# First four row tiles of x in four pieces of the contraction, w1 ahead of w2, three w sums on GpSimd

## The chip, the cores and the metric

The kernel runs on one core of a Trainium2 chip. The metric is the device time of one execution in microseconds (us). Before the change three runs took 298.63, 298.87 and 299.97 us; the median, 298.87 us, is the number to be forecast for the changed kernel.

## The reference

```python
def setup_inputs():
    batch, m, k, n = 16, 512, 1024, 768
    return {
        "x": np.random.randn(batch, m, k).astype(np.float32),
        "w1": np.random.randn(k, n).astype(np.float32),
        "w2": np.random.randn(k, n).astype(np.float32),
    }

def reference(x, w1, w2):
    y1 = np.matmul(x, w1)
    y2 = np.matmul(x, w2)
    return (np.tanh(y1) * y2).astype(np.float32)
```

Seen as one matrix, x has 8192 rows, that is 64 row tiles of 128 rows, with a contraction of 1024, that is 8 pieces (k = 0 to 7) of 128. Both w1 and w2 have 768 columns. Everything is multiplied in 16-bit floats and summed in 32-bit floats.

## The kernel before

**Blocks.** In the code `u` is w1 and `v` is w2; `u3` is the 128 contraction rows k = 3 of w1, 128 partitions by 768 columns, 384 KB. The columns of the result are cut into three blocks of 512: `a` is columns 0 to 511 of x·w1, `b` is columns 0 to 511 of x·w2, and `G` holds the last 256 columns of both, side by side. One matmul instruction multiplies a 128x128 piece of transposed x with 128x512 of w and adds into one of the eight banks of PSUM; four of them (half of the contraction) are a slot.

**The head.** The first four row tiles (`HEAD = 4`) are computed plainly: for each tile eight matmuls for `a`, eight for `b`, eight for `G`, 88 in all, because the `b` block of tile 3 is kept back and done as the last thing of the kernel. The head exists to give TensorE work while w1 and w2 are still arriving. Its row tiles come by four loads of 512 KB in 32-bit floats (`y0` to `y3`, lines 411 to 415), are cast to 16 bits (line 417), transposed by TensorE, eight 128x128 transposes for a tile (line 460), and copied out of PSUM into tiles `xT` in two halves of 512 columns (line 465).

**The rest.** The other 60 row tiles are done as 20 triples. In a triple the three tiles' two contraction halves are six x blocks, named by bits: 1 and 2 are the halves of the first tile, 4 and 8 of the second, 16 and 32 of the third. The six w blocks are named the same way: 1, 2, 4 are `a`, `b`, `G` of contraction half 0 (k = 0 to 3), and 8, 16, 32 are `a`, `b`, `G` of half 1 (k = 4 to 7). A table of sums and differences lets 15 products do the work of 18. `A_SUMS` are sums of x blocks, one VectorE instruction on 128x512 16-bit values each (line 507), made anew for each triple. `B_SUMS` are eleven sums of w blocks, one VectorE instruction on 128x2048 16-bit values each (line 497), made once and kept. `C_OPS` is the list of products (`p0` to `p14`, four matmuls each, line 550), of copies and additions between PSUM banks and SBUF, and of the tanh and multiply at the end. The first triple needs the w sums first.

**The planner.** `Planner` lays out all operations by a list schedule: each has a duration for each engine that may do it, a due time, and what it needs. The matmuls of the head may be put in any order that fits; the products run in the fixed order `plan.strict`. The first triple's products of this order are, before the change, p7 p1 p6 p10 p9 p12 p8 p11 p14, then p7 of the second triple, then p0 and p13 of the first. The order that the planner finds is pinned: each engine's instructions run in it, and each queue issues its loads in it.

**Loads.** `SP_LOADS` and `ACT_LOADS` are the orders in which SyncE and ScalarE issue the loads of the four row tiles and of the sixteen pieces of w. Row tiles 4, 5 and 6, and after them all others, are loaded by GpSimd's queue with a cast on the way (line 471). The first of these is held back by a `gate`, a one-element GpSimd copy that reads a freshly landed w piece (`POOL_LOADS = "5.0:v5 ..."` waits for v5); later ones are paced by `gate_x`, a one-element GpSimd copy of transposed x (line 586). Tiles 4, 5 and 6 are transposed by TensorE, those from 7 on by a DMA transpose on SyncE's queue (line 474). Every piece of w is cast to 16 bits by ScalarE or VectorE (lines 427 and 429).

**Warm-up.** Before the first load lands, TensorE multiplies constants (`WARM`), and at four places that are named by hand (`FILLERS`) it does so again in a wait of the head.

Of the kernel before, what the change touches and what calls it, by code (L numbers as in the profile page):

```python
# [85 lines left out]
MUL_DUE = 0.022  # L86
MARGIN = {"S": 0.407, "B": 0.262, "T": 5.87, "L": 9.71, "early": 0.060}
# [3 lines left out]
FILLERS = {"PT1.0": (512,), "m1b2": (192,), "m1b7": (256,), "PT2.1": (448,)}  # L91
# [5 lines left out]
SP_LOADS = ("y0 y1 v7 u3 y2 u1 v4 u0 v0 "  # L97
            "v1 v3 u2 u4 v5 v6 u6 u5 u7")
ACT_LOADS = "y3 v2"
POOL_LOADS = "5.0:v5 4.0 4.1 5.1 6"  # L100


class Planner:
# [221 lines left out]
    def spare(self, n):  # L325

        t = self.start_of[n]
        return [b for b in range(len(self.held)) if all(t <= a or z <= t - 1.0 for a, z in self.held[b])][0]
# [3 lines left out]
def kernel(  # L332
# [7 lines left out]
    nc = tc.nc  # L340
# [19 lines left out]
    XF_BUFS, XG_BUFS = 3, max((SP_LOADS + ACT_LOADS).count("y"), 1)  # L360
# [13 lines left out]
    xtpool = pool("xt", XT_BUFS)  # L374
# [15 lines left out]
    xt_last = once.tile([P, KO, P], f16, name="xT_last")  # L390
# [7 lines left out]
    xgpool = head_stack.enter_context(tc.tile_pool(name="xg", bufs=XG_BUFS))  # L398
# [12 lines left out]
    def load_x32(e, mt, halves):  # L411
        if mt not in x32:
            x32[mt] = xfpool.tile([P, K], f32, tag="xf", name="x_f")
        at = slice(halves[0] * F, (halves[-1] + 1) * F)
        pin(engine[e].dma_start(x32[mt][:, at], xf[mt][:, at]))  # L415

    def cast_y(e, mt):
        xhs[mt] = xgpool.tile([P, K], f16, tag="xh", name="xh")
        copy(e, xhs[mt], x32[mt])
# [27 lines left out]

    def xt_tile(mt):
        if mt not in xts:
            xts[mt] = xt_last if mt == HEAD - 1 else xtpool.tile([P, KO, P], f16, tag=f"xT{mt % 3}", name="xT")  # L450
        return xts[mt]

    def transpose_32(e, mt, h, chain):
        for k in range(KH):
            pin(nc.tensor.transpose(bank(chain)[:, k * P:(k + 1) * P], x32[mt][:, (h * KH + k) * P:(h * KH + k + 1) * P], ident))

    def evacuate_32(e, mt, h, chain):
        copy(e, xt_tile(mt)[:, h * KH:(h + 1) * KH, :].rearrange("p k m -> p (k m)"), bank(chain))
# [9 lines left out]
    def load_x(e, mt, lo, n):  # L468
        if mt not in xhs:
            xhs[mt] = (xgpool if mt < HEAD else xhpool).tile([P, K], f16, tag="xh", name="xh")  # L470
        pin(nc.gpsimd.dma_start(xhs[mt][:, lo * P:(lo + n) * P], xf[mt][:, lo * P:(lo + n) * P]))  # L471
# [7 lines left out]
    def abs_x(e, mt):  # L479
        abs_sum(e, xhs[mt] if mt in xhs else x32[mt], mt)  # L480
# [18 lines left out]
    def x_operand(i, v):  # L499
        if v & (v - 1):  # L500
            return ss[i, v]
        bit = v.bit_length() - 1
        return xts[HEAD + 3 * i + bit // 2][:, bit % 2 * KH:(bit % 2 + 1) * KH, :]
# [15 lines left out]
    def mm(e, chain, mt, k, c, lo, n):  # L519
        begun[chain] = begun.get(chain, 0) + 1  # L520
        w = w_columns(k, c, lo, n)
        pin(nc.tensor.matmul(shaped(bank(chain)[:, lo:lo + n], w), xts[mt][:, k, :], w, start=begun[chain] == 1, stop=begun[chain] == KO, skip_group_check=True))  # L522

    def plain_tanh(e, mt, lo, n, chain):
        pin(nc.scalar.activation(out_tile(mt)[:, lo:lo + n], bank(chain)[:, :n], ACT.Tanh))
# [59 lines left out]
    def gate_x(e, mt):  # L585
        pin(nc.gpsimd.tensor_copy(held_x, xts[mt][:, 0, :1]))  # L586

    def gate(e, c, k):
        pin(nc.gpsimd.tensor_copy(held, (x32[k] if c == "y" else wfs[c, k])[:, :1]))
# [7 lines left out]
    K_ORDER = [4, 5, 6, 7, 0, 1, 2, 3]  # L597

    head = PE_HEAD.split()
    head_at = {entry: HEAD_START + n * SLOT for n, entry in enumerate(head)}  # L600
    ORIGIN = HEAD_START + (len(head) - 15) * SLOT
# [25 lines left out]
    parts, early, last, back = {}, set(), "", []  # L627
    both = sorted([(ISSUE_ACT * z, "act", z, n) for z, n in enumerate(act_loads)] + [(ISSUE_SP * z, "sp", z, n) for z, n in enumerate(sp_loads)])
    issuer, last_on = {}, {"act": "", "sp": ""}
    for _, e, z, n in both:  # L630
# [3 lines left out]
        if n[1] == "y":  # L634
            mt = int(n[2])
            op(n, {e: (0.49, 0.49) if e == "sp" else (ISSUE_ACT, 0.5) if n != act_loads[-1] else (ISSUE_ACT + TABLE, 0.5)}, -100, [], load_x32, mt, (0, 1), issued=[last], behind=back[-WF_BUFS:][:1] if len(back) >= WF_BUFS else [],
               dma=(e, 1.295 + more, 1.15, 0.75, 0.159))
            op(f"cy{mt}", {"dve": (0.6, 0.69), "act": (0.92, 1.02)}, None, [n], cast_y, mt)
            back.append(f"cy{mt}")
            for h in range(2):  # L640
                parts.setdefault(mt, []).append((h * KH, KH))
                op(f"PT{mt}.{h}", {"pe": (0.25, 0.25)}, None, [f"cy{mt}"], transpose_16, mt, h * KH, KH, ("T", mt, h), chains=[("T", mt, h)])
                op(f"T{mt}.{h}", {"dve": (0.36, 0.45), "act": (0.51, 0.6)}, None, [f"PT{mt}.{h}"], evacuate_16, mt, h * KH, KH, ("T", mt, h), chains=[("T", mt, h)])
                early.add(f"T{mt}.{h}")
        elif n[1] == "x":
# [334 lines left out]
```

## Time and profile before

| what | value |
|---|---|
| runs (us) | 298.63, 298.87, 299.97; median 298.87 |
| span of the profiled execution, first to last instruction | 297.3 us |
| median less that span | 1.6 us |
| TensorE busy | 290.9 us, 98% of the span |
| VectorE busy | 255.5 us, 86% |
| ScalarE busy | 227.6 us, 77% |
| GpSimd busy | 46.7 us, 16% |

The profiled execution has no time of its own in the list of runs; its span stands beside the median, and the 1.6 us between them lie ahead of the first and behind the last instruction, as far as the two executions are alike. The span counts from its first instruction, and all places in the trace are given in us from there. PE is TensorE, PEld its loads of the stationary operand, DVE VectorE, ACT ScalarE, POOL GpSimd, SP SyncE. A row of the timeline has its start, its length, the engine, the line, the operation with output and input, and how many instructions it merges; in brackets stands how long the engine had been idle before it and what ended that. Matmuls are pipelined, so the length of one is longer than the distance to the next.

### The profile page before, as it was taken

What the parts mean: (1) busy time and instruction counts of PE and PEld (TensorE: products, weight loads), DVE (VectorE), ACT (ScalarE), POOL (GpSimd) and SP (SyncE); (2) the same over time, 40 slices, a digit from 0 to 9 for tenths busy, and PEclk for the clock granted to TensorE, in tenths of its full rate; (3) what the DMA queues carried; (4) which work ended last, traced back from release to release, by engine and by line L of the source; (5) the groups of instructions that cost most, each with busy time, mean ns of one, the idle gap of its engine ahead of it and who ended that gap; (6) DMA issues with size and microseconds to landing.
All of it is one profiled execution on the core that took longest, in us unless ns stands there. A gap on an engine that the chain in (4) does not pass through costs nothing.

```text
span 297.3 us, 4698 instructions
## 1 busy us (share of the span) xinstructions
PE 290.9 (98%) x1419; PEld 137.7 (46%) x1419; DVE 255.5 (86%) x517; ACT 227.6 (77%) x450; POOL 46.7 (16%) x122
## 2 busy tenths in 40 slices
PE   6999999999999999999999999999999999999995
PEld 3545444444444675444444444444444444444443
DVE  1458999999988999898899988989899898999685
ACT  3798988996969769697876979788696866867561
POOL 1024040211030111113121010212101030000000
PEclk9999999999999999999999999999999999999999
DMA  7999999999999999999999999999989899681316
GB/s 263 406 403 230 162 169 222 242 251 258 110 317 212 221 255 244 221 215 259 161 227 217 172 223 199 246 224 215 226 169 245 164 279 244 144 240 47 119 55 215
DMA packets 82827, 64.55 MB, mean 217 GB/s; under 512 B 62704, under 2 KB 64752, under 8 KB 82800
## 3 DMA queue, kind: packets, MB, share of 16 engines
q1 hardware_dynamic: 73584, 47.59, 62.6%
q0 software_dynamic: 8928, 15.73, 34.3%
q10 hardware_dynamic: 288, 0.92, 0.8%
q8 instruction: 11, 0.18, 0.3%
q14 instruction: 16, 0.13, 0.1%
HBM read 39.85 MB, written 25.17 MB: 219 GB/s over the span
## 4 chain that ended last, share of the span: by engine, by line
PE 91%; DMA 6%; ACT 1%; SPq 0%; DVE 0%; issue 0%
PE bank L550 87%; DMA w_f<-in_w_dram 4%; PE bank L522 3%; DMA x_f<-in_x_dram 2%; ACT wh L427 1%; PE bank L463 1%; SPq L423 0%; DVE o_last L529 0%; SPq L415 0%; PE bank L580 0%
## 5 line engine op out<-in xcount | busy, mean ns | idle before, releaser
L550 PE MATMUL bank<-b,s 128*128 128x512 f16 (+1 forms) x664 | 148.1, 371 | 0.0
L550 PEld LDWEIGHTS <-s 128*128 128x128 f16 x832 | 81.2, 98 | 91.4 <-DVE s L507 0.6
L553 ACT ACTIVATE s<-bank 128x512 f32<-128x512 f32 x100 | 58.6, 595 | 41.0 <-PE bank L550 40.5
L560 DVE TENSOR_TENSOR bank<-bank,s 128x512 f32<-128x512 f32 x100 | 69.5, 697 | 18.1 <-PE bank L550 7.8
L477 ACT ACTIVATE junk<-xh 128x1024 f16<-128x1024 f16 x64 | 67.3, 1051 | 0.2
L567 DVE TENSOR_TENSOR o<-o,bank 128x512 f32<-128x512 f32 (+1 forms) x120 | 63.1, 548 | 2.5 <-ACT o L563 1.7
L550 PEld LDWEIGHTS <-xT 128*128 128x128 f16 x412 | 40.3, 98 | 46.1 <-ACT xT L427 0.2
L550 PE MATMUL bank<-b,xT 128*128 128x512 f16 (+1 forms) x252 | 58.5, 369 | 0.0
L563 ACT ACTIVATE o<-bank 128x256 f32<-128x256 f32 (+1 forms) x80 | 33.0, 432 | 12.4 <-PE bank L550 6.1
L550 PE MATMUL bank<-wh,s 128*128 128x512 f16 (+1 forms) x168 | 41.1, 369 | 0.0
L550 PE MATMUL bank<-wh,xT 128*128 128x512 f16 x160 | 40.9, 379 | 0.0
L586 POOL COPY held_x<-xT 128x1 f16<-128x1 f16 x52 | 12.2, 235 | 165.1 <-DMA xT<-xh 165.0
L471 POOL DMA_DIRECT2D xh<-in_x_dram x62 | 33.3, 540 | 20.3 <-issue 6.6
L507 DVE TENSOR_TENSOR s<-s,xT 128x512 f16<-128x512 f16 x80 | 32.3, 421 | 1.2
L563 ACT ACTIVATE o<-s 128x512 f32<-128x512 f32 x40 | 24.9, 623 | 1.2 <-DVE s L560 1.2
L507 DVE TENSOR_TENSOR s<-xT 128x512 f16<-128x512 f16 x60 | 25.0, 418 | 0.0
L553 ACT ACTIVATE bank<-bank 128x512 f32<-128x512 f32 x40 | 21.7, 573 | 1.6 <-DVE bank L560 0.9
L522 PE MATMUL bank<-wh,xT 128*128 128x512 f16 x72 | 18.8, 378 | 0.3
L507 DVE TENSOR_TENSOR s<-xT,s 128x512 f16<-128x512 f16 x40 | 16.7, 417 | 0.0
L560 DVE TENSOR_TENSOR bank<-s,bank 128x512 f32<-128x512 f32 x20 | 13.9, 694 | 1.6
L560 DVE TENSOR_TENSOR s<-s,bank 128x512 f32<-128x512 f32 x20 | 13.6, 681 | 0.3 <-ACT s L553 0.3
L477 ACT ACTIVATE junk<-wh 128x768 f16<-128x768 f16 x16 | 13.5, 842 | 0.2
(42 smaller groups left out, 120.6 us busy)
## 6 DMA issues: line engine op xcount, KB each, us to landing
out_dram<-o SPq DMA_DIRECT2D x54, 384.0 KB, 4.7
xh<-in_x_dram POOLq DMA_DIRECT2D x58, 256.0 KB, 5.7
w_f<-in_w_dram SPq DMA_DIRECT2D x15, 384.0 KB, 6.3
out_dram<-o SPq DMA_DIRECT2D x9, 256.0 KB, 2.0
x_f<-in_x_dram SPq DMA_DIRECT2D x3, 512.0 KB, 4.7
out_dram<-o SPq DMA_DIRECT2D x9, 128.0 KB, 1.7
xT<-xh SPq DMA_TRANSPOSE x57, 5.3
x_f<-in_x_dram ACTq DMA_DIRECT2D x1, 512.0 KB, 4.9
```

Of the source, the lines that this page charges most:

```text
L427: pin(nc.scalar.copy(dst, src))
L463: pin(nc.tensor.transpose(b[:, (k - lo) * P:(k - lo + 1) * P], xhs[mt][:, k * P:(k + 1) * P], ident_h))
L471: pin(nc.gpsimd.dma_start(xhs[mt][:, lo * P:(lo + n) * P], xf[mt][:, lo * P:(lo + n) * P]))
L477: pin(nc.scalar.activation(junk[:, :src.shape[-1]], src, ACT.Abs, scale=scale, accum_out=sums[:, column:column + 1]))
L507: pin(engine[e].tensor_tensor(ss[i, v], x_operand(i, a), x_operand(i, b), OP[how]))
L522: pin(nc.tensor.matmul(shaped(bank(chain)[:, lo:lo + n], w), xts[mt][:, k, :], w, start=begun[chain] == 1, stop=begun[chain] == KO, skip_g ...
L550: pin(nc.tensor.matmul(to, x_operand(i, a)[:, k, :], w, start=begins and k == 0, stop=k == KH - 1, skip_group_check=True))
L553: pin(nc.scalar.activation(place(i, dst, True), place(i, src), ACT.Copy, scale=float(sign)))
L560: pin(nc.vector.tensor_tensor(d, a, b, ALU.add if signs == (1, 1) else ALU.subtract))
L563: pin(nc.scalar.activation(out_tile(HEAD + 3 * i + r)[:, lo:lo + n], place(i, src)[:, :n], ACT.Tanh, scale=float(sign)))
L567: pin(nc.vector.tensor_tensor(o, o, place(i, src)[:, at:at + n], ALU.mult))
L586: pin(nc.gpsimd.tensor_copy(held_x, xts[mt][:, 0, :1]))
```

## The change

The four row tiles of the head are no longer loaded tile by tile. A load `q0` to `q3` now brings two of the eight contraction pieces (256 columns, 1 KB of each row) of all four tiles together, 512 KB as before; one cast makes 16 bits of it, eight transposes turn it, and one copy of 1024 columns brings it out of PSUM for all four tiles. So the head can use a piece of w for all four tiles as soon as the matching `q` is there. The loads come in a new order: q0 and q2 early, q1 and q3 behind the first six pieces of w1, and all of w1 but u6 and u1 ahead of w2; v7 and v6 are last. The gate of the row tiles from 4 on waits for v3. The head's `G` is split in `U` (w1's last 256 columns) and `V` (w2's), 256 columns each, two row tiles to a bank. Three of the eleven w sums, 26 = 2 − 24, 37 = 1 − 36 and 27 = 29 − 6, go from VectorE to GpSimd. The products of the first triple begin with p1 and p6 in place of p7. All transposed x lies in one tile with the same number of places as before. The planner's margins are new, and the filling multiplications are put by rule wherever the plan has a wait.

```diff
-PE_HEAD = ("1a0 0a1 1b1 0b1 1G1 p7 p1 0a0 3a0 2b1 p6 0G0 2a1 1b0 1G0 3a1 "
-           "p10 3G1 0b0 p9 p12 2G1 p8 1a1 p11 p14 2b0 0G1 3G0 2G0 2a0")
-HEAD_START = 2.5
+PE_HEAD = ("1a1 p1 p6 0U1 0a1 2a0 3V0 1U0 1V0 3a0 3U1 1a0 2U1 0U0 3V1 p7 p10 2V1 2V0 p9 0V0 0a0 1b0 "
+           "2U0 1U1 0b0 2a1 1b1 p12 p8 3U0 2b1 p11 3a1 2b0 0V1 p14 0b1 1V1")
+HEAD_START = 14.142
...
-MUL_DUE = 0.022
-MARGIN = {"S": 0.407, "B": 0.262, "T": 5.87, "L": 9.71, "early": 0.060}
+MUL_DUE = 2.735
+MARGIN = {"S": 1.925, "B": 0.146, "T": 14.795, "L": 4.568, "early": 0.268}
...
-FILLERS = {"PT1.0": (512,), "m1b2": (192,), "m1b7": (256,), "PT2.1": (448,)}
...
-SP_LOADS = ("y0 y1 v7 u3 y2 u1 v4 u0 v0 "
-            "v1 v3 u2 u4 v5 v6 u6 u5 u7")
-ACT_LOADS = "y3 v2"
-POOL_LOADS = "5.0:v5 4.0 4.1 5.1 6"
+SP_LOADS = "u5 q2 u4 u0 u7 u2 q1 q3 v2 u6 v0 u1 v1 v3 v4 v5 v7 v6"
+ACT_LOADS = "q0 u3"
+XQ, XQ32, XQ_GROUPS = (2, 2, 2, 2), (), 1
+POOL_B = (26, 37, 27)
+POOL_LOADS = "4.1:v3 6 5.1 5.0 4.0"
...
+    def fillers(self, until):
+        found, busy = {}, None
+        for n in sorted((n for n in self.ops if self.engine_of[n] == "pe"), key=lambda n: self.start_of[n]):
+            t = self.start_of[n]
...
+            if busy is not None and t - busy > 0.32 and self.spare(n):
+                found[n] = self.spare(n)[0], int((t - busy - 0.12) * 600) // 32 * 32
+            busy = t + self.ops[n]["engines"]["pe"][0]
+        return found
...
+    xt_all = once.tile([P, HEAD + 3 * (XT_BUFS - 1), KO, P], f16, name="xT")
...
+    def load_q(e, j):
+        k, w = xq_at[j]
+        x32[j] = xfpool.tile([P, HEAD, w * P], f32, tag="xf", name="x_f")
+        pin(engine[e].dma_start(x32[j], xf[:HEAD].rearrange("mt p k -> p mt k")[:, :, k * P:(k + w) * P]))
+
+    def cast_q(e, j):
+        k, w = xq_at[j]
+        copy(e, xh_head[:, :, k * P:(k + w) * P], x32[j])
...
+    def transpose_q(e, j, g, chain):
+        k, w = xq_at[j]
+        n = HEAD // XQ_GROUPS
+        b = bank(chain) if j in XQ32 else bank(chain).bitcast(f16)
+        for mt in range(n):
+            for z in range(w):
+                src = x32[j][:, g * n + mt, z * P:(z + 1) * P] if j in XQ32 else xh_head[:, g * n + mt, (k + z) * P:(k + z + 1) * P]
+                pin(nc.tensor.transpose(b[:, (mt * w + z) * P:(mt * w + z + 1) * P], src, ident if j in XQ32 else ident_h))
+
+    def evacuate_q(e, j, g, chain):
+        k, w = xq_at[j]
+        n = HEAD // XQ_GROUPS
+        b = bank(chain) if j in XQ32 else bank(chain).bitcast(f16)
+        copy(e, xt_all[:, g * n:(g + 1) * n, k:k + w, :], b[:, :n * w * P].rearrange("p (t k m) -> p t k m", t=n, k=w))
...
+    def mm(e, chain, mt, k, c, lo, n, at, count):
         begun[chain] = begun.get(chain, 0) + 1
+        col = N * (c in "bV") + F * (c in "UV") + lo
+        pin(nc.tensor.matmul(bank(chain)[:, at:at + n], xt_tile(mt)[:, k, :], wh[:, k, col:col + n], start=begun[chain] == 1, stop=begun[chain] == count, skip_group_check=True))
...
     for v, a, b, how in B_SUMS:
-        op(f"B{v}", {"dve": DVE_B}, None, w_needs(a) + w_needs(b), w_sum, v, a, b, how)
+        op(f"B{v}", {"pool": (4.6, 4.7)} if v in POOL_B else {"dve": DVE_B}, None, w_needs(a) + w_needs(b), w_sum, v, a, b, how)
...
+    fillers = plan.fillers(24.0)
```

More of the change, by code (lines that the diff above doesn't have):

```diff
@@ L711 @@
[L711 removed]
+                took = MM if n == F else MM / 2
+                op(name, {"pe": (took, took)}, head_at[f"{mt}{c}{k // KH}"] + z % KH * took, [f"c{'uv'[c in 'bV']}{k}", part(mt, k)],
+                   mm, chain, mt, k, c, 0, n, lo, KO if c in "ab" else 2 * KO, chains=[chain])
+                plain[c, mt].append(name)
+            xt_readers[mt] += plain[c, mt]
+    for c in "aUbV":
+        for mt in range(HEAD):
+            if (c, mt) not in plain:
+                continue
```

157 lines of the change are left out of this document (77 added, 80 removed).

## The prediction

> **What bounds the kernel now.** I read the page first, then the chain of waits, then the timeline of the first 45 us. The page's first and fourth parts say that TensorE is busy for 98% of the span and makes 91% of the chain that ended last. In the chain in order of time (start, length, what; the second fence) no other engine and no transfer releases TensorE after 22.98:
>
> ```profile
> span 297.3 us, 4698 instructions
> ...
> PE 290.9 (98%) x1419; PEld 137.7 (46%) x1419; DVE 255.5 (86%) x517; ACT 227.6 (77%) x450; POOL 46.7 (16%) x122
> ...
> PE 91%; DMA 6%; ACT 1%; SPq 0%; DVE 0%; issue 0%
> ```
>
> ```profile
> 22.98 3.40 PE bank L522 x15
> ...
> 36.63 242.78 PE bank L550 x1168
> 279.41 0.01 PE bank L580
> 279.42 12.97 PE bank L550 x60
> 292.38 1.76 PE bank L522 x16
> ```
>
> The 1168 products from 36.63 on include 44 extra ones (the sixth triple's eleven products that do not begin a bank are cut in halves), so they are 1124 matmuls of 512 columns: 0.216 us each. Nothing is left to win there. Only the head can move, and a delay in it goes to the end undiminished. The rows of the head:
>
> ```profile
> 9.16 0.38 PE L522 MATMUL bank<-wh,xT 128*128 128x512 f16 x1
> ...
> 12.45 0.62 PE L463 MATMUL bank<-ident_h,xh 128*128 128x128 f16 x8
> ...
> 24.12 0.56 DVE L429 CAST wh<-w_f 128x768 f16<-128x768 f32 x1 [0.90 <-DMA w_f<-in_w_dram]
> ...
> 26.38 0.40 PE L463 MATMUL bank<-ident_h,xh 128*128 128x128 f16 x4
> ...
> 40.66 1.55 PEld L550 LDWEIGHTS <-xT 128*128 128x128 f16 x8 [0.18 <-DMA xT<-xh]
> 40.82 1.03 PE L550 MATMUL bank<-wh,xT 128*128 128x512 f16 x4
> ...
> 41.68 1.03 PE L550 MATMUL bank<-b,xT 128*128 128x512 f16 x4
> ```
>
> The first matmul on data starts at 9.16. By 36.47 TensorE has done the 88 plain matmuls and four products, 104 matmuls, or 22.5 us, and 32 transposes of 0.056 us (0.45 us of spacing for eight), 1.8 us. The stretch is 27.3 us, so TensorE waited 3.0 us in it, filling partly with constants. The product at 41.68 is p0 of the first triple, the one with a single x block against a w sum (27); the one before it, at 40.82, is p7 of the second triple, which just found its transposed x tile. I use 41.68 as the anchor: p0 needs sum 27, and the order of products is fixed, so what p0 loses the kernel loses.
>
> **The head's gain.** Transfers go at one rate whatever the order:
>
> ```profile
> 4.00:6.00 2.00, 1.21 (x4) 0.53 (x2) 0.10 (x1) 0.30 (x1) 0.00 (x0) 1.00 1.02 416
> ...
> 18.00:20.00 2.00, 2.00 (x10) 0.88 (x9) 1.70 (x2) 1.97 (x6) 0.00 (x0) 1.00 1.03 399
> ```
>
> ```profile
> out_dram<-o SPq DMA_DIRECT2D x9, 256.0 KB, 2.0
> out_dram<-o SPq DMA_DIRECT2D x9, 128.0 KB, 1.7
> ```
>
> ```profile
> 7.95 0.69 DVE L429 CAST xh<-x_f 128x1024 f16<-128x1024 f32 x1
> ```
>
> (First two stretches of 2 us, whose last number is GB/s; then two stores with their us from issue to landing; then a cast of a row tile.) Before, y0, y3, y1 and v2 (1.97 MB) lay ahead of the cast at 7.95 or beside it. After, q0, u5, q2 and u3 (1.84 MB) come first, so q2 with u5 is there at about 7.8. Then follow the cast 0.69, eight transposes 0.62, and one copy of 1024 columns, about 0.8 on VectorE: the first matmul at 9.9, that is **+0.75**. From there each piece of w1 gives 4 x 1.5 matmuls, 1.3 us, while 384 KB at 400 GB/s take 0.98 us. u5, u4 and u0 keep TensorE busy for 3.9 us, to 13.8. The next piece needs q1, the seventh load on SyncE's queue. By bytes it lands at about 13.1, and with its cast, transposes and copy it is usable at 15.3: of these 1.5 us the transposes take 0.45, and 1.0 is waiting. q3 follows inside the work of u3 and u2. Waiting falls from 3.0 to 1.0, **-2.0**. Eight more transposes fall behind the first matmul, **+0.45**, and 64 matmuls of 256 columns at 0.110 (1.76 for 16) in place of 32 at 0.216 cost **+0.1**. Together -0.7: without anything else p0 comes at 41.0. Bounds: all waiting gone and the start kept, -2.5; the start late by another 1 us and the waiting kept, +2.
>
> The four q loads have rows of 1 KB in place of 4 KB. No load of before has such rows; the stores above with 1 KB and 2 KB rows differ by 0.3 us for 128 KB more, so 1 KB rows do not stand out. I take +0.1 us a load, 0.4 in all (0 to 3). The casts of w, 16 before and after, and the four abs sums are moved, not multiplied. All loads are still 20, and the gate's piece, v3, stands at the same place behind 15 others, so row tiles 4 to 9 start as before plus 0.4. The one tile for all transposed x has the same ten places, and pieces of `wh`, one tile too, are already read here while others are written: nothing.
>
> **The three sums on GpSimd.** This step decides. By the new order v6 lands last, and 24 and 36 both contain w2's second half; 26 = 2 - 24, 37 = 1 - 36 and 27 = 29 - 6 (29 = 5 - 24) come after them. So none of the three can start before the last cast, 24.12 + 0.56 + 0.4 = 25.1. What the trace shows of GpSimd beside VectorE (first all gate copies, their ns as minimum/median/maximum; then rows of the timeline):
>
> ```profile
> L586 POOL COPY held_x<-xT x52: 187/188/1035, 39.9 to 250.2; 128x1 f16<-128x1 f16 x52
> ```
>
> ```profile
> 1.61 0.29 POOL L865 CAST ident_h<-ident 128x128 f16<-128x128 f32 x1
> ...
> 24.78 2.36 DVE L497 TENSOR_TENSOR b<-wh 128x2048 f16<-128x2048 f16 x2
> ...
> 32.14 0.53 POOL L471 DMA_DIRECT2D xh<-in_x_dram  x1 [5.49 <-PE bank L550]
> ...
> 33.11 0.42 DVE L507 TENSOR_TENSOR s<-s,xT 128x512 f16<-128x512 f16 x1
> 33.45 0.42 DVE L507 TENSOR_TENSOR s<-s,s 128x512 f16<-128x512 f16 x1
> ...
> 42.11 1.22 DVE L497 TENSOR_TENSOR b<-b,wh 128x2048 f16<-128x2048 f16 x1
> 42.34 1.03 POOL L586 COPY held_x<-xT 128x1 f16<-128x1 f16 x1 [0.53 <-DMA xT<-xh]
> ...
> 87.89 0.42 DVE L507 TENSOR_TENSOR s<-xT,s 128x512 f16<-128x512 f16 x1
> 88.03 0.33 POOL L586 COPY held_x<-xT 128x1 f16<-128x1 f16 x1 [1.19 <-DMA xT<-xh]
> ```
>
> A one-element copy takes 0.188 us in the median, also beside VectorE's operations on PSUM. Beside the w sum of 42.11 it takes 1.03 and ends at 43.37, the sum at 43.33; beside the x sum of 87.89 it ends at 88.36, the x sum at 88.31. So GpSimd does not read beside a VectorE instruction with two SBUF inputs; it gets its turn when that has ended. The other direction, VectorE behind a long GpSimd instruction, the trace cannot show. Bounds: VectorE waits not at all, or for all of it. I take the second, because the rows show the path handed over whole. The GpSimd sum's length is not shown either: at least VectorE's 1.18 (2.36 for two); by the only GpSimd cast, 0.29 for 128 columns, 16 times as much, 4.6. Leaving out the 0.19 that even one element costs gives 1.8 for one input, 3.5 for two. I take 4.6.
>
> [...]
>
> The sum: before p0 these must pass one after another, in whatever order, all after 25.1: on VectorE the w sums 24, 36, 18 and 29, 4 x 1.18 = 4.7; on GpSimd three, 13.9; the nine x sums of products p1 to p14 (3, 11, 15, 31, 34, 35, 10, 21, 63), at 0.34 apart, or some 0.45 where one reads the other's result, 3.8. That is 22.4, so p0 comes at 47.5 and not 41.0. Against 41.68 it is **+5.8**: span 303.1, and with the median's 298.87 a time of **304.7**. Queued behind a blocked x sum on VectorE are the additions and multiplications that free the banks, so TensorE, out of plain matmuls at about 32, waits for p1, p6 and p9. Three sums fewer on VectorE give it 3.6 us, already in the sum.
>
> **Rivals.**
> (A) VectorE does not wait for GpSimd. Then GpSimd's three sums, 13.9 from 26.3, end at 40.2, just ahead of p0 at 41.0: the head's gain stays, 298.2. For it: no row shows VectorE waiting for GpSimd. Against it: the copies show exclusion to the end of an instruction. It is this case if p6 starts by 34.
> (B) As A, but the second triple's p7 is held by its transposed x, 40.66 before, now later by the 0.4 of the q loads: the gain is lost, +0.4, 299.3. Against it: GpSimd's next x load, issued at 32.14 before, is now behind a sum, so the transposes have the queues to themselves.
> (C) Not slower, and more than A: the three sums slip between VectorE's PSUM operations at little cost, and q1's wait closes, first matmul at 9.4 with under 0.2 us of waiting: -2.1, 296.8. It needs GpSimd sums near 2 us. Only the 1.8 us end speaks for that.
> (D) The sums do not get on GpSimd's path in the planned order, since one-element gates stand between them and wait for transposes; the third then starts 3 us later: 307.7.
>
> **How the numbers follow.** Forecast 0.50, D 0.08, A 0.19, B 0.11, C 0.12. The forecast's own range is 301.3 (sums of 3.5 us, 3 x 1.1 less) to 307 (VectorE's PSUM operations of that stretch not overlapped: some 2 to 3 us more). To leave out no more than 2 in 10 the range must reach A and part of C: 297.2 to 307.7. One measurement of this kernel can't tell less than 0.5%, 1.5 us, from no change. Slower by more than that: forecast and D, 0.58. Within: A, B and a little of C, 0.28. Faster: the rest of C and a late A, 0.14.
>
> **What would show it.** First matmul on data near 9.9, a wait near 14 ended by q1's copy. GpSimd rows L497 of 4 to 5 us each between 26 and 45, and beside them VectorE x sums (L507) stretched or starting only when such a row ends; TensorE waits of 2 to 5 us between 32 and 48, released by L507 or by GpSimd's L497; p0 near 47. Wrong would be: x sums of 0.42 us inside a GpSimd sum, or p0 at 41.

## The result and the profile after

| | before | after |
|---|---|---|
| median (lowest to highest) | 299.16 us (298.63 to 299.97) | 310.30 us (309.06 to 311.98) |
| ratio, 95% interval | | 1.0374 [1.0335, 1.0412] |
| profiled execution, its span | | 310.11 us, 308.5 us |

The change costs 11.1 us where 5.8 were forecast, and 310.30 us lies above the range, which ends at 307.7. Executions that ran slow as a whole (two of e1, one each of e4, e5, e10 and e13) are left out of the ratios and of the times given below, which are medians of the others, while the expectations quote medians of all. First the page of the kernel after: the span, TensorE's granted clock in 40 slices, the pieces of program loaded, the chain that ended last.

```profile
span 308.5 us, 4734 instructions
...
PEclk9599999999999999999999999999999999999998
...
q8 instruction: 12, 0.20, 0.3%
...
PE 87%; DVE 8%; DMA 2%; issue 1%; ACT 0%; SPq 0%; DVEq 0%
```

VectorE has come into the chain with 8%, where it had 0%. The second digit of the clock is a 5. `q8` is the queue on which pieces of program come, twelve of them with 0.20 MB, so about 16 KB each; before there were eleven (`q8 instruction: 11, 0.18, 0.3%`), a difference that matters at the end. Now the timeline of the kernel after (start, length, engine, line, operation; in brackets how long the engine had been idle, and for whom):

```profile
9.86 1.89 PE L478 MATMUL bank<-ident_h,xh_head 128*128 128x128 f16 x16 [3.94 <-ACT xh_head L439]
...
12.50 5.80 PE L548 MATMUL bank<-wh,xT 128*128 128x512 f16 x24
...
18.13 1.17 PE L896 MATMUL bank<-ones 128*128 128x512 f32 x4
...
25.54 0.56 DVE L441 CAST wh<-w_f 128x768 f16<-128x768 f32 x1 [0.76 <-DMA w_f<-in_w_dram]
...
28.00 8.51 POOL L523 TENSOR_TENSOR b<-wh,b 128x2048 f16<-128x2048 f16 x2
...
32.68 1.02 DVE L441 COPY xT<-bank 128x1024 f16<-128x1024 f16 x2 [4.11 <-PE bank L489]
...
34.28 2.52 DVE L533 TENSOR_TENSOR s<-xT 128x512 f16<-128x512 f16 x1
...
37.86 1.04 PE L576 MATMUL bank<-b,s 128*128 128x512 f16 x4 [1.92 <-DVE s L533]
...
42.81 4.17 POOL L523 TENSOR_TENSOR b<-b,b 128x2048 f16<-128x2048 f16 x1 [4.55 <-DVE b L523]
...
44.16 3.09 DVE L533 TENSOR_TENSOR s<-xT 128x512 f16<-128x512 f16 x1
...
48.93 1.03 PE L576 MATMUL bank<-b,xT 128*128 128x512 f16 x4
```

Four things stand here. The first transposes wait until 9.86, for q2, though q0 was cast by VectorE at 6.99: in TensorE's pinned order q2's come first. The first data matmul comes at 12.50, not 9.9. The fillers of 18.13 run in a wait that is not there, since the cast of q1 that they were to cover ended long before. And the two x sums of 34.28 and 44.16 take 2.52 and 3.09 us, six and seven times their 0.42: they end at 36.80 and 47.25, just behind the GpSimd sums, which end at 36.51 and 46.98. That is the direction that the trace of before could not show: the x sum is held until the GpSimd instruction has ended. "The lock" is my name for this from here on. p0 of the first triple starts at 48.93, 7.25 us later than before.

The clock, by stretches of 2 us (start:end, then length, busy time of the five engines, granted clock, DMA share, GB/s):

```profile
10.00:12.00 2.00, 2.00 (x17) 1.98 (x16) 0.91 (x2) 1.61 (x3) 0.00 (x0) 0.50 1.03 387
...
14.00:16.00 2.00, 2.00 (x7) 0.91 (x6) 0.00 (x0) 1.34 (x2) 0.00 (x0) 0.50 1.07 383
16.00:18.00 2.00, 2.00 (x14) 1.26 (x13) 0.00 (x0) 1.85 (x3) 0.00 (x0) 1.00 1.04 403
```

After 3.94 us of idling TensorE runs at half its clock (0.50 granted) until 16: 7 matmuls in the last 2 us of it, 14 in the next, at 1.00.

The chain of waits in order of time, from TensorE's entry into unbroken work on; then the end of the kernel, the transfers after 285 us (issues, KB each, median us to landing):

```profile
56.95 231.64 PE bank L576 x1116
...
303.35 0.42 DVE o_last L555
```

```profile
q8 instruction: 2, 0.03, 0.7%
...
out_dram<-o_last SPq DMA_DIRECT2D x2, 128.0 KB, 3.8
```

Before, VectorE's last instruction started at 294.17; now at 303.35: 9.2 us are lost by then, 7.25 of them at p0 and another 1.9 between p0 and 56.95, where the chain runs through VectorE, thrown back by the x sum of 44.16. From its end to the end of the span it was 297.3 - 294.6 = 2.7 us and is 308.5 - 303.8 = 4.7: another 2.0 us, because the last two stores land 3.8 us after issue instead of 1.8. So three suspects have to be told apart, the GpSimd sums, the head and the tail, and VectorE's last instruction is the mark by which I compare runs below.

### The profile page after: what moved, and what is told of

It is laid out like the page before. It is cut to its first block, busy times and chain, and to the rows that moved or that the text cites. A ratio compares the mean times of both kernels' runs of the same rounds, so it can differ in the third digit from the quotient of the medians.

```text
span 308.5 us, 4734 instructions
## 1 busy us (share of the span) xinstructions
PE 294.4 (95%) x1451; PEld 142.6 (46%) x1451; DVE 252.1 (82%) x512; ACT 228.9 (74%) x448; POOL 58.0 (19%) x125
## 4 chain that ended last, share of the span: by engine, by line
PE 87%; DVE 8%; DMA 2%; issue 1%; ACT 0%; SPq 0%; DVEq 0%
PE bank L576 79%; PE bank L548 6%; DVE s L533 3%; DMA x_f<-in_x_dram 2%; DVE bank L586 1%; DVE b L523 1%; DVE o L555 1%; PE bank L896 1%; PE bank L478 1%; DVE xT L441 0%; DVE o L593 0%; DVE s L586 0%; ACT xh_head L439 0%; PE bank L489 0%; DVE o_last L555 0%
## 5 line engine op out<-in xcount | busy, mean ns | idle before, releaser
L503 ACT ACTIVATE junk<-xh 128x1024 f16<-128x1024 f16 x60 | 63.0, 1050 | 0.3
L576 PEld LDWEIGHTS <-xT 128*128 128x128 f16 x412 | 40.3, 98 | 45.8
L612 POOL COPY held_x<-xT 128x1 f16<-128x1 f16 x52 | 11.5, 221 | 161.4 <-DMA xT<-xh 161.3
L576 PE MATMUL bank<-wh,xT 128*128 128x512 f16 x160 | 40.9, 379 | 0.0
L533 DVE TENSOR_TENSOR s<-xT 128x512 f16<-128x512 f16 x60 | 28.6, 496 | 0.8 <-DMA xT<-xh 0.8
L548 PE MATMUL bank<-wh,xT 128*128 128x256 f16 (+1 forms) x136 | 24.4, 332 | 0.0
L548 PEld LDWEIGHTS <-xT 128*128 128x128 f16 x136 | 13.7, 103 | 8.4 <-issue 1.9
L441 DVE COPY xT<-bank 128x1024 f16<-128x1024 f16 (+1 forms) x7 | 4.2, 613 | 15.7 <-PE bank L478 11.6
```

What stands on the lines that cost most here:

```text
L441: pin(engine[e].tensor_copy(dst, src))
L503: pin(nc.scalar.activation(junk[:, :src.shape[-1]], src, ACT.Abs, scale=scale, accum_out=sums[:, column:column + 1]))
L533: pin(engine[e].tensor_tensor(ss[i, v], x_operand(i, a), x_operand(i, b), OP[how]))
L548: pin(nc.tensor.matmul(bank(chain)[:, at:at + n], xt_tile(mt)[:, k, :], wh[:, k, col:col + n], start=begun[chain] == 1, stop=begun[chain] ...
L576: pin(nc.tensor.matmul(to, x_operand(i, a)[:, k, :], w, start=begins and k == 0, stop=k == KH - 1, skip_group_check=True))
L612: pin(nc.gpsimd.tensor_copy(held_x, xt_tile(mt)[:, 0, :1]))
```

## Experiments

**Each suspect by itself.** Theory L: the GpSimd sums and the lock set p0. Rival H: the head (late first transposes, half the clock, fillers) sets it.

e1, all w sums on VectorE, planned anew:

```diff
-POOL_B = (26, 37, 27)
+POOL_B = ()
```

> The changed kernel with all w sums on VectorE again, everything else of the change kept; the planner lays the order out anew. Theory L (the three GpSimd sums and the lock set p0 of the first triple): p0 comes at about 43 to 44 (the time before, 41.7, plus the 2 us or so by which the new head is late), TensorE is released by VectorE's x sums for less than 1 us after 36, and the time is 302 to 304 us, 6 to 8 below the changed kernel's 310.3. Rival H (the new head is the cost: the first transposes at 9.9, half the clock from 8 to 16, fillers where nothing waits): the time stays above 307, p0 still comes after 47.

Measured 308.47 us, ratio 1.0307 [1.0268, 1.0347]: only 1.8 less, where L had 6 to 8; H had said above 307. The planner's order is another one here, so the run mixes two things; its profile is from an execution of 312.76 us, and I read nothing from it. What the next expectation for this edit says of ScalarE and transposed tiles in it is therefore not shown.

e2, the other way round: the kernel before, with the three sums on GpSimd and nothing else edited; this too is planned anew.

```diff
-        op(f"B{v}", {"dve": DVE_B}, None, ...
+        op(f"B{v}", {"pool": (4.6, 4.7)} if v in (26, 37, 27) else {"dve": DVE_B}, None, ...
```

> The kernel before with nothing but the sums 26, 37 and 27 put on GpSimd, planned at 4.6 us each. Theory L: VectorE instructions with two SBUF inputs are stretched to the end of a GpSimd sum, p0 of the first triple (41.68 before) comes at 46 to 48, the time is 303 to 306 us. Rival H: GpSimd finishes its sums beside VectorE, p0 at 42 to 43, the time 299 to 300.5.

Measured 310.28 us, 1.0367 [1.0326, 1.0408]. The three sums, with the new plan that comes with them, cost the old kernel 11 us, as much as the whole change; L had 303 to 306, and p0 at 46 to 48 where it comes at 51.40. Its timeline and then its clock:

```profile
26.75 8.61 POOL L497 TENSOR_TENSOR b<-wh,b 128x2048 f16<-128x2048 f16 x2
...
28.77 2.67 DVE L507 TENSOR_TENSOR s<-xT 128x512 f16<-128x512 f16 x1 [0.34 <-ACT xT L427]
31.55 4.09 DVE L507 TENSOR_TENSOR s<-s,xT 128x512 f16<-128x512 f16 x1
...
36.69 3.57 PE L550 MATMUL bank<-b,s 128*128 128x512 f16 x8 [4.69 <-DVE o L529]
...
38.04 4.27 DVE L507 TENSOR_TENSOR s<-xT 128x512 f16<-128x512 f16 x1
...
43.81 1.02 PE L550 MATMUL bank<-wh,xT 128*128 128x512 f16 x4 [2.27 <-DVE o L529]
```

```profile
36.00:38.00 2.00, 1.31 (x4) 0.47 (x4) 2.00 (x4) 0.31 (x1) 0.13 (x1) 0.50 0.96 104
...
40.00:42.00 2.00, 1.54 (x4) 0.44 (x3) 2.00 (x1) 0.00 (x0) 2.00 (x2) 0.50 0.23 50
```

Three x sums of 0.42 take 2.67, 4.09 and 4.27; TensorE waits 4.69 us, then works at half clock (0.50) until near 42, then waits 2.27 more. The wait that dropped the clock is paid for again in the work after it: the eight matmuls of 36.69 take 3.57 us, eight at 60.03 take 1.89. The tail is 2.7 us here (span 307.0, last VectorE instruction at 303.85), as before.

e3, TensorE kept busy through the wait for q2:

```diff
-WARM = (512, 512, 256)
+WARM = (512, 512, 256, 512, 512, 512, 512)
```

> The changed kernel with four more constant matmuls of 512 columns ahead of the first transposes, so that TensorE is busy from 1.3 to about 9.4 instead of 5.9. If the idle time of 3.9 us is what halves the clock, the granted clock stays at 1.0 from 10 to 16, the first 16 transposes take 0.9 us instead of 1.9 and plain matmuls of 512 columns come 0.216 apart instead of 0.43. Theory H: those 2.7 us or so reach the end, 307 to 308 us. Theory L: TensorE only runs out of plain matmuls 2 us sooner and waits for the same x sums behind the same GpSimd sums, which start after the last w cast; 309.5 to 311. If the clock halves at a fixed time, whatever TensorE does, the windows stay at 0.5.

e4, no constants after the first 6 us:

```diff
-    fillers = plan.fillers(24.0)
+    fillers = {}
```

> The changed kernel without the constant matmuls that it puts ahead of late work after the first 6 us (six records, about 1.9 us of TensorE's time where the data they wait for has long landed). Theory H: 1.5 to 2 us less at the end, 308 to 309 us. Theory L: the time gained is waited for at p1, behind the first GpSimd pair; 309.5 to 311.

Measured 310.76 us (1.0408 [1.0336, 1.0481]) and 311.12 us (1.038 [1.0331, 1.0428]): no gain. The windows and the timeline of e3:

```profile
10.00:12.00 2.00, 2.00 (x23) 1.50 (x22) 1.35 (x3) 1.61 (x3) 0.00 (x0) 1.00 1.02 387
...
38.00:40.00 2.00, 1.73 (x5) 0.63 (x6) 1.90 (x6) 0.29 (x2) 0.12 (x1) 0.53 0.60 74
```

```profile
38.27 1.89 PE L576 MATMUL bank<-b,s 128*128 128x512 f16 x4 [4.97 <-DVE s L533]
```

The clock stays at 1.00 in the head, from 6 to 18, so it was the idling that halved it. But p1 starts at 38.27, as late as in the changed kernel: what the head gains is waited for behind the same x sum (4.97 us in place of 1.92), and the longer wait halves the clock there (0.53). In e4 it is the same, p1 at 38.41 after 5.27 us. H falls as long as the GpSimd sums are there. Idling of 3.94 and 4.97 us dropped the clock here, and one of 1.92 us in the changed kernel, before 37.86, did not (1.00 from 36 to 44). But in e6, below, TensorE fell to about half its speed near 39 after two waits of 1.48 and 0.60 us with 1.1 us of work between them, so the length of a single wait doesn't tell when the clock drops.

**The sums against the same order.** Since a new plan is a change of its own, e5 keeps the plan of the changed kernel to the last instruction and lets VectorE do the three sums at their places. e6 leaves them on GpSimd in four instructions each; e7 adds to e5 the edits of e3 and e4; e8 is e5 without fillers, with the transfers of q0 and q2 exchanged and two more constants.

In `w_sum`, e5 and then e6; in `load_q`, e8:

```diff
-        pin(engine[e].tensor_tensor(*blocks, OP[how]))
+        pin(nc.vector.tensor_tensor(*blocks, OP[how]))
```

```diff
+        if e == "pool":
+            for k in range(KH):
+                pin(nc.gpsimd.tensor_tensor(*[z[:, k:k + 1] for z in blocks], OP[how]))
+            return
```

```diff
+        j = {0: 2, 2: 0}.get(j, j)
         k, w = xq_at[j]
```

> The changed kernel in exactly its planned order, with the three sums 26, 37 and 27 issued by VectorE at the same places of the order instead of by GpSimd (the run with the sums on VectorE and a new order stayed at 308.9, held by ScalarE's abs sums and late transposed x tiles). Theory L (the lock sets p0): no x sum takes over 0.5 us, sum 26 fills VectorE's idle time before 32, p1 starts within 0.5 us after TensorE runs out of plain matmuls, p0 comes at 43 to 45, the time is 302 to 305 us. Rival X (the later transposed x tiles and ScalarE's abs sums hold the first triples anyway): p0 still comes after 47 and the time is 307 to 310.

> The changed kernel with each of the three GpSimd sums issued as four instructions of 512 columns, about 1.05 us each, in place of one of 2048 columns of 4.2 us. If VectorE waits for the GpSimd instruction that has begun, and gets its turn when it ends, an x sum is stretched by at most about 1.1 us and not by 2.1 to 4; p1 comes 1 to 2 us sooner, the time is 306 to 309 us. If GpSimd keeps its turn from one piece to the next, the x sums are stretched as now and the time stays at 309.5 to 311.

> As the run with the sums on VectorE in the same order, and TensorE kept busy by four more constant matmuls to 9.4, and no fillers after that. Without the GpSimd sums nothing hides the head any more, so half clock and needless fillers should now reach the end: 2 to 4.5 us below that run. If they change nothing here either, the transposed x tiles or ScalarE set the end.

> As the run before it (sums on VectorE in the same order, no fillers), with the transfers of the pieces q0 and q2 exchanged, so that q2, whose transposes come first in TensorE's order, is on ScalarE's queue and lands first, near 6.2; two constant matmuls more instead of four. The first transposes start near 7.4, the first data matmul near 10.0 instead of 11.3, TensorE's clock stays up. If the head sets the end, 0.5 to 1.5 us below the run before; if not, the same.

| | us | ratio, 95% interval | last VectorE instruction |
|---|---|---|---|
| changed kernel | 310.30 | 1.0374 [1.0335, 1.0412] | 303.35 |
| e5, same order, sums on VectorE | 307.03 | 1.0271 [1.025, 1.0293] | 299.92 |
| e6, GpSimd in pieces | 310.28 | 1.0379 [1.0354, 1.0404] | 303.54 |
| e7, e5 with warm clock, no fillers | 307.33 | 1.0262 [1.0216, 1.0307] | 301.66 |
| e8, e5 with q2 first, no fillers | 306.24 | 1.0235 [1.0216, 1.0255] | 299.74 |

Taking the sums from GpSimd gives 3.3 us, although VectorE has 3.5 us more to do. It isn't the 6 to 8 of theory L, and e5's timeline shows why:

```profile
26.47 0.56 DVE L441 CAST wh<-w_f 128x768 f16<-128x768 f32 x1 [1.83 <-DMA w_f<-in_w_dram]
...
32.79 0.42 DVE L533 TENSOR_TENSOR s<-xT 128x512 f16<-128x512 f16 x1
...
34.29 1.03 PE L576 MATMUL bank<-b,s 128*128 128x512 f16 x4
...
40.38 1.22 DVE L523 TENSOR_TENSOR b<-b,b 128x2048 f16<-128x2048 f16 x1
...
42.26 3.64 PE L576 MATMUL bank<-b,s 128*128 128x512 f16 x16 [1.79 <-DVE bank L586]
...
47.47 1.03 PE L576 MATMUL bank<-b,xT 128*128 128x512 f16 x4
```

The x sum takes 0.42 again, and p1 starts at 34.29 with no wait of TensorE before it; p6, the next product, waits 0.77 us at 36.19 for an x sum. But p0 comes at 47.47, and TensorE's last wait, before 42.26, is for an addition on PSUM (41.52 to 42.2) at the end of a row of VectorE instructions that is unbroken from 31.18 on. In the kernel before the same product started at 36.47, behind the addition of 35.59. Laid beside each other, the two rows of VectorE differ by 6.0 us: the last cast of w comes 2.35 later (26.47 for 24.12); between it and the addition stand seven w sums instead of five, 2.3 us, one of them sum 27 at 40.38, which before came behind the addition; and three copies of transposed row tiles, 1.35, which before were all ScalarE's in this stretch. x sums are nine in both. These three differences are read from the rows; no run takes one of them away alone.

e7 and e8 agree from TensorE's side: the first data matmul comes at 11.46 and 10.30 in place of 12.12 (e7's first 16 transposes take 1.05 us where e5's take 1.68, and e8's granted clock is 1.00 from 8 to 14), and TensorE still enters its unbroken work at 42.24 and 41.69. (The profile of e7 lost 1.7 us more near 260, to a transposed tile.) So without the GpSimd sums TensorE's head does not set the end either, but for 1 us at most: e8 is 0.8 us below e5, and of e7's four executions two took 306.1 us and two 308.6.

e6 shows when the lock ends; its timeline:

```profile
28.08 9.93 POOL L525 TENSOR_TENSOR b<-wh,b 128x512 f16<-128x512 f16 x8
...
34.67 2.33 DVE L537 TENSOR_TENSOR s<-xT 128x512 f16<-128x512 f16 x2
...
37.03 1.72 DVE L537 TENSOR_TENSOR s<-s,xT 128x512 f16<-128x512 f16 x2
```

VectorE got its turn between the pieces: pairs of x sums take 2.33 and 1.72 us, about one piece each, instead of one x sum 2.52. p1 comes 0.8 us sooner (37.06 for 37.86). But GpSimd's pair takes 9.93 instead of 8.51, and TensorE, which waits 1.48 us before p1 and 0.60 before p6, works at about half its speed from 38.81 to near 42 (its four matmuls at 40.24 take 1.91 us, those at 37.06 took 1.04; the page's clock is 7 tenths in the slice from 38.6 to 46.3); p0 comes at 49.93, and the time is the same. What pieces would give at full clock is therefore open.

**The tail.** All profiles with the new head have twelve pieces of program and a tail of 4.5 to 5.2 us; the four with the old head and eleven pieces (before, e2, e12, e14) have 2.7 or 2.8. e9 makes TensorE's program in the kernel before as long as that of the changed kernel.

```diff
-WARM = (512, 512, 256)
+WARM = (512, 256)
...
+    for z in range(36):
+        pin(nc.tensor.matmul(banks[2][:, :32], ident_h, ident_h[:, :32], start=True, stop=True))
```

> The kernel before with 36 tiny constant matmuls of 32 columns (and their 36 weight loads) ahead of the first transposes in place of 512 columns of the constant matmuls there, so that TensorE's program is as long as that of the changed kernel (2979 instructions against 2908 before and 2972 after). In the profiles with the new head a twelfth 16 KB piece of program is loaded among the last stores, which land 2 us later behind it; in the two with the old head there are eleven. If that is what lengthens the tail by 2 us: twelve pieces, the last stores land about 3.5 us after issue instead of 1.8, the time is 300.5 to 301.5 us. If the tail has another cause: 298.5 to 299.5.

Measured 302.57 us, 1.011 [1.0074, 1.0147], 1 us above the range for twelve pieces (two executions near 301.6, two near 303.6). The transfers after 285 us:

```profile
q8 instruction: 1, 0.02, 0.4%
...
out_dram<-o_last SPq DMA_DIRECT2D x2, 128.0 KB, 2.7
```

A twelfth piece comes (the page of e9 counts 12), and the last store lands behind it: the tail is 301.9 - 297.6 = 4.3 us, 1.6 more than before. So the longer program is the cause of 1.6 of the tail's 2.0 us. The rest of e9's loss is ahead of the tail, as VectorE's last instruction starts 3.0 later than before in its profile, of an execution of 303.52 us; the edit moved the head too, and p7 of the second triple waited 1.42 us for its transposed x tile at 43.80.

**VectorE's chain.** Left are 5.8 us of e5, by which p0 is later than before (47.47 for 41.68). Theory V: VectorE's work up to the addition of 41.52 sets the end. Rival: late row tiles, TensorE's order, or ScalarE.

e10, an edit on e8; e11, on e10; e13, on e5 (it leaves out three quarters of four w sums; a line not shown sets their tiles to zero at the start):

```diff
     def evacuate_16(e, mt, lo, n, chain):
+        e = "act"
```

```diff
     order = plan.run()
+    order.remove("B27")
+    order.insert(order.index([n for n in order if n[:3] == "add"][1]) + 1, "B27")
```

```diff
+        if v in (37, 18, 29, 27):
+            blocks = [z[:, :1] for z in blocks]
         pin(nc.vector.tensor_tensor(*blocks, OP[how]))
```

> As the run with q2 first (sums on VectorE in the same order; 306.24), with the five copies that bring the transposed row tiles 4 to 6 out of PSUM all on ScalarE; three of them were VectorE's, 1.4 us. Theory V (VectorE's chain from the first row tile to the product near 42 sets the end): 1 to 1.5 us less, 304.7 to 305.3. Rival: the transposed tiles, TensorE's order or ScalarE set it: no less, 306 to 307.

> As the run before it, and sum 27 (1.14 us) is moved behind the two additions on PSUM that stood behind it in VectorE's order; only p0, some 5 us later, reads it. Theory V: another 1.0 to 1.2 us less, 303.6 to 304.3. Rival: no change.

> The changed kernel in its planned order with the sums on VectorE (307.2), where the four w sums 37, 18, 29 and 27, which stand between the first row tiles' copies and the product near 42.3, are computed for 512 of their 2048 columns only (the rest stays zero), about 0.35 us each in place of 1.18. Theory V (VectorE's chain sets the end): the product that started at 42.26 starts 2.5 to 3.3 us sooner, near 39.3, and the time is 304.0 to 304.8 us. Rival T (late row tiles, TensorE's order of transposes, ScalarE): under 1 us sooner, 306.3 to 307.3.

e10: 306.63 us (1.0262 [1.0241, 1.0282]), no gain. ScalarE does the copies between its abs sums, so the last of the first x sums starts at 33.36, after 1.41 us of waiting for ScalarE: the cost went to another engine. e11: 305.89 us (1.023 [1.0213, 1.0247]), 0.7 less, where V had 1.0 to 1.2; but the intervals of the two just meet, and in e11's profile the last w cast came 1.6 us later than in e10's (27.17 for 25.54), which hides the effect there. It speaks for V, and settles nothing. e13: 305.40 us (1.0215 [1.0184, 1.0247]), 1.6 less than e5 where V said 2.4 to 3.2 and the rival under 1. Its timeline says where the rest went:

```profile
39.58 0.70 DVE L588 TENSOR_TENSOR bank<-bank,s 128x512 f32<-128x512 f32 x1 [1.56 <-ACT s L581]
...
40.33 3.68 PE L578 MATMUL bank<-b,s 128*128 128x512 f16 x16 [1.04 <-DVE bank L588]
...
45.58 1.03 PE L578 MATMUL bank<-b,xT 128*128 128x512 f16 x4
```

TensorE's last wait ends at 40.33 instead of 42.26, and p0 comes 1.9 us sooner. VectorE, freed of most of the four sums, then waits 1.56 us itself for ScalarE, whose copy stands behind abs sums, each the sum of the absolute values of one row tile (`junk`). So VectorE's chain sets the end in e5 by 1.9 us, and below that ScalarE does, with 3.9 us of p0's delay left. Its rows in the kernel before and in e13, each time the last abs sum of the first four row tiles and the first copy of a product out of PSUM:

```profile
23.86 1.05 ACT L477 ACTIVATE junk<-xh 128x1024 f16<-128x1024 f16 x1
...
34.12 0.58 ACT L553 ACTIVATE s<-bank 128x512 f32<-128x512 f32 x1
```

```profile
36.73 1.06 ACT L503 ACTIVATE junk<-xh_head 128x1024 f16<-128x1024 f16 x1
...
38.97 0.58 ACT L581 ACTIVATE s<-bank 128x512 f32<-128x512 f32 x1
```

Before, the four abs sums of the first tiles lie between casts of w, from 16.98 on, and three of later tiles stand between 30.63 and the copy. With the new head such a sum needs all four q loads and no longer the one load of its tile, and the planner puts it behind the casts: in e13 the four lie at 30.45, 31.64, 33.19 and 36.73 (in the changed kernel at 32.32, 33.51, 35.06 and 38.60), and seven abs sums stand ahead of the copy. Four more at 1.18 us are 4.7 us, and the copy is 4.85 later. No run moves them, so this part is read from the rows and not tested.

**The order of w alone.** e14 leaves the first tiles and the sums of the kernel before and puts w1 ahead of w2; it too is planned anew.

```diff
-SP_LOADS = ("y0 y1 v7 u3 y2 u1 v4 u0 v0 "
-            "v1 v3 u2 u4 v5 v6 u6 u5 u7")
+SP_LOADS = ("y0 y1 u7 u3 y2 u1 u4 u0 u2 "
+            "u6 u5 v7 v4 v5 v0 v1 v3 v6")
-POOL_LOADS = "5.0:v5 4.0 4.1 5.1 6"
+POOL_LOADS = "5.0:v0 4.0 4.1 5.1 6"
```

(A filler is left out where no bank is free.)

> The kernel before with the loads of w reordered alone, all pieces of w1 (but the one that ScalarE's queue had) ahead of those of w2, all sums on VectorE, first row tiles as before, planned anew. Theory V: VectorE has one cast and most of its w sums left after the last w2 piece near 24.5, its chain reaches 2 to 4 us further and TensorE waits for it between 33 and 42; 300.5 to 303 us, without the lengthened tail. Rival T: the order of the w loads costs nothing by itself, since as many bytes have landed by 24.5; 298.5 to 299.7.

Measured 303.25 us, 1.0136 [1.0113, 1.016]: 4.3 us for the order of w with its own plan, without the longer tail (2.7 us). The timeline, from the first w sums and the last cast of w on:

```profile
23.88 2.36 DVE L497 TENSOR_TENSOR b<-wh 128x2048 f16<-128x2048 f16 x2
24.08 0.83 ACT L427 CAST wh<-w_f 128x768 f16<-128x768 f32 x1
...
39.11 3.64 PE L550 MATMUL bank<-b,s 128*128 128x512 f16 x16 [1.46 <-DVE bank L560]
...
45.70 1.04 PE L550 MATMUL bank<-wh,s 128*128 128x512 f16 x4 [0.35 <-DVE s L507]
```

The last w piece is cast as early as before (24.08 against 24.12), so the bytes are not late. But none of the eleven w sums starts before 23.88, where the kernel before had made three by then (18.86, 20.62, 22.00): three more, 3.4 us, left to the engine that TensorE then waits for, at 39.11 and again at 45.70. The first of these waits is not VectorE's alone: the chain of e14 leads from it over a product at 36.63 to ScalarE's first copy of a product, at 36.00 where it was at 34.12, again behind one abs sum more. p0 comes at 44.32, 2.6 us late; the other 1.8 us are lost behind it, where the chain runs through three w sums of VectorE from 40.23 on. The changed kernel, whose order of w is not quite this one, has made two of the eleven before its last cast.

**GpSimd beside VectorE in mid-kernel.** e12 puts one idle GpSimd instruction of 2048 columns into each of sixteen triples of the kernel before: an addition in the first eight, and in the others a copy, to see whether one input holds an x sum too.

```diff
+            if n[:3] == "p6." and 3 <= int(n[3:]) <= 18:
+                if int(n[3:]) <= 10:
+                    pin(nc.gpsimd.tensor_tensor(steady["z"], wsum[5], wsum[6], ALU.add))
+                else:
+                    pin(nc.gpsimd.tensor_copy(steady["z"], wsum[5]))
```

> The kernel before, with one GpSimd instruction of 2048 columns added to each of sixteen triples in the middle, its result used by nobody: in triples 3 to 10 an addition of two f16 tensors, in triples 11 to 18 a copy of one. Lock on two-input work: beside the additions (about 4.2 us each) x sums of VectorE take up to 4 us instead of 0.42. [...] No claim on the time.

The timeline at one addition and one copy:

```profile
97.08 4.08 POOL L875 TENSOR_TENSOR z<-b,b 128x2048 f16<-128x2048 f16 x1
...
97.87 3.58 DVE L507 TENSOR_TENSOR s<-xT,s 128x512 f16<-128x512 f16 x1
...
240.04 2.25 DVE L507 TENSOR_TENSOR s<-xT,s 128x512 f16<-128x512 f16 x1
...
240.10 1.91 POOL L877 COPY z<-b 128x2048 f16<-128x2048 f16 x1
```

Beside the additions x sums took 2.28 us (at 84.15), 3.58 (at 97.87) and up to 4.6. The x sum of 240.04, which fell into a copy, was held too: it took 2.25 us and ended 0.3 us behind the copy's end. So a GpSimd copy of one input held an x sum as an addition did, only the copy is 1.91 us long and the addition 4.08. VectorE's instructions with an input in PSUM were not held: one of 0.69 us at 82.81, inside the addition that starts at 82.06, takes 0.69 as elsewhere. The one execution took 317.72 us, 19 us more for sixteen instructions whose result nobody reads; two of the page's 40 slices show a lower clock in it (7 and 5 tenths).

Not tried: the four pieces with w1 and w2 loaded by turns. In that arrangement the first four tiles hold six of the eight banks for w1 alone, and w2 would want as many at the same time. So the pieces' own cost is open, but for what their loads cost (below).

## Why the prediction was wrong, point by point

**The account.** Of 11.1 us, the tail is 2.0 (e9 reproduces 1.6 of it). GpSimd instead of VectorE for the three sums is 3.3 (e5): p0 at 48.93 for 47.47, and 1.9 behind p0. The remaining 5.8 stand in e5 as p0 at 47.47 for 41.68. There VectorE's row is longer and later: a last cast of w 2.35 later, one w sum more behind it, sum 27 at a place that was planned for GpSimd, and three copies. That VectorE sets the end is shown by e13 for 1.9 of the 5.8; for the other 3.9 ScalarE is as late, by its rows because of the four moved abs sums. e14 shows the same two engines at work with the order of w and a new plan alone (4.3 us in the old kernel). The parts don't add: alone in the old kernel the sums cost 11 (e2), with a plan of its own and some 6 us at half clock.

**The step that failed** is the head's gain: "Together -0.7: without anything else p0 comes at 41.0." Without the GpSimd sums p0 comes at 47.47 (e5), and at 45.58 with most of four sums cut out (e13). I had counted TensorE's waits and the transfers, VectorE's work behind the last cast only inside the chain of sums shared with GpSimd, as if it cost nothing unless GpSimd took part, and ScalarE's abs sums as "moved, not multiplied", at nothing. By my own terms VectorE's work was 8.5 us from 25.1 on, ending at 33.6; I left out that it can't start as a block: VectorE sits idle for 4.11 us before 32.68 in the changed kernel, since its x sums need row tiles whose transposes TensorE does later, and then has three copies of these tiles to do as well.

**The time.** 310.30 is 5.6 us above 304.7. p0 came 1.4 later than 47.5. "What p0 loses the kernel loses" failed by 1.9: from p0 to VectorE's last instruction it is 252.5 us before, in e5 and in e13, and 254.4 in the changed kernel. The tail's 2.0 were in no term, and the kernel before took 299.16 beside it and not 298.87. That p0 fell so near 47.5 is luck: the chain was to run unbroken from 25.1, and it began at 28.00 with VectorE idle for 4.11 us; of p0's 7.25 the GpSimd sums are 1.5, and the rest was put at nothing.

**First data matmul at 9.9, +0.75:** wrong, 12.50. q2 was cast by ScalarE in 1.04 us, from 8.76 on, sixteen transposes went ahead and not eight, and at half clock they took 1.68 us where e3 needs 0.9. Yet it cost nothing at the end (e3, e4), and 1 us at most without the GpSimd sums (e7, e8): TensorE's head was no longer the bound.

**Waiting falls by 2.0:** the waits went, but the planned fillers stayed in their place. Also without effect.

**GpSimd sums:** none before 25.1 was right (28.00); 4.6 us each was 4.2 to 4.3; VectorE blocked to the end of the GpSimd instruction was right, and was the forecast's bet. Of the waits of 2 to 5 us between 32 and 48 there was one, of 1.92 before p1. The sum itself was mis-sized: 5.8 us were put on that chain of sums, and it costs 3.3 against VectorE doing the sums; 4 us of the first pair lie in VectorE's idle time.

**The last stores** were nowhere in the sum: I counted the 64 matmuls of 256 columns in place of 32 as +0.1 of TensorE's time, and not as 32 instructions more, with a weight load each, that have to be loaded. The transposes are 56 in both kernels.

**Rivals.** A (VectorE does not wait) is refuted by the rows above. B did not occur: p7 found its tile. C is out with it. D named a late third sum; it came late, at 42.81, but for VectorE's sum 29 (4.55 us of waiting on `DVE b`), not for gates. **q loads** at +0.1 each were taken too low: the last cast of w starts at 25.54, 1.4 later than before's 24.12. Transfers did not go at one rate: in stretches of 1 us they moved 302 to 383 GB/s from 3 to 8 and 349 to 374 from 11 to 15, while q loads were under way, where the kernel before has 373 to 418 and 396 to 409. By 16 that is 0.41 MB less, 1.0 us at 400 GB/s, and e14, with the old loads of row tiles, moves as much as the kernel before (266 and 406 GB/s in the first two of the page's 40 slices, before 263 and 406, the changed kernel 243 and 380). Whether the rows of 1 KB are the reason no run separates; and why the last cast came as late as 26.47 in e5 and 27.17 in e11 is open.

## What to carry to other kernels

A load order is also the order in which sums can be made: before moving one weight ahead of another, count the instructions that come to stand behind the last piece, on every engine and not only on TensorE. Work put on GpSimd is not off VectorE's path where VectorE has instructions with two SBUF inputs; here each x sum that met a GpSimd sum waited to its end (2.52 to 4.27 us in place of 0.42, changed kernel and e2). When two parts of a change hold the path in parallel, undo each in the exact order of instructions of the whole: a new plan moved e1 by 1.4 us against e5.

## What the runs showed of the hardware

- A GpSimd copy with one SBUF input (1.91 us for 2048 16-bit columns) held a VectorE addition of two SBUF inputs, 2.25 us in place of 0.42 (e12); GpSimd additions with two inputs (4.08 us in e12) held them so that they took up to 4.6. Where both ends can be read, the hold ended 0.3 us behind the GpSimd instruction (changed kernel, e12). VectorE instructions with an input in PSUM were not held (0.69 us inside an addition, e12).
- Idling of 3.94 to 4.97 us put TensorE at half clock (0.50 to 0.53 granted) for 3 to 6 us afterwards (changed kernel, e2, e3), and waits of 1.48 and 0.60 us close together in e6 were followed by 3 us at about half speed. So the wait of 4.69 us in e2 cost at least 6.4, with the 1.7 that the eight matmuls behind it took longer. Keeping TensorE busy with constants kept the clock at 1.00 (e3), but the time stayed (310.76 for 310.30): constants are of no use where another engine sets the end.
- Program came in pieces of about 16 KB (0.18 MB in eleven, 0.20 in twelve). 64 recorded matmuls and weight loads more (2838 to 2902) brought a twelfth, and the last stores landed 3.8 us after issue instead of 1.8; in the kernel before, lengthened in the same way, 2.7 (e9).
